# The first chunk of a projection made 384 tokens instead of 320, with five of the first loads issued by GpSimd

## The chip, the cores and the metric

The kernel runs on one core of one Trainium2 chip. The metric is the device time of one execution in microseconds (us). Before the change it is 463.41 us, the median of three runs (463.18 to 463.77).

## What is computed

One decoder layer over 1024 prompt tokens and 64 sample tokens (8 sequences of 8), 1088 tokens in all, with 1024 model columns. Cut to what matters here:

```python
def mixer_layer(x, conv_buf, S0, norm_g, w_in, ...):
    h = rms_norm(x, norm_g)
    proj = jnp.einsum('btd,de->bte', h, w_in.astype(h.dtype))
    a, gl, zc, q, k, v, zg, lr = jnp.split(proj, SPLIT_POINTS, axis=-1)
    u = a * jax.nn.sigmoid(gl)
    cv, new_buf = depthwise_causal_conv(u, conv_buf, conv_w, conv_b)
...
    out = jnp.einsum('bte,ed->btd', jnp.concatenate([cv, o], axis=-1), w_out.astype(x.dtype))
    return x + out, new_buf, S
```

The change concerns the start: the RMSNorm of x, and the first four of the projection's 128-column tiles, gl and a, each for convolution channels 0 to 127 and 128 to 255.

## The kernel before

**Tiling.** Tokens lie along the free dimension in three chunks, `CHUNKS = [(0, 384), (384, 384), (768, 320)]`; the last holds 256 prompt tokens and all 64 sample tokens. The 1024 model columns are eight groups of 128 partitions, k = 0 to 7. Each fp32 operand is split into a high and a low part (`hh` and `hl` for the normed x, `h_...` and `l_...` for weights), and a product is three matmuls: high by high, low by high, high by low. One weight tile over one chunk is so 8 x 3 = 24 matmuls into one PSUM bank (`proj_chunk`).

**The start.** `FIRST = 2`: the chunk of 320 tokens is taken first, and in a special way. Its x is multiplied by the norm's gain and split at once (`raw_split`, two instructions per k: one of ScalarE, one of VectorE), without the root mean square, which `rms_scale` works out beside it and which is multiplied onto the results afterwards. So TensorE can begin as soon as x for k = 0 and the first weights are there. Four weight tiles (gl and a for channel tiles 0 and 1; in the text gl0, a0, gl1, a1) are loaded in halves of four k each; the first half of each comes in two pieces of two k (128 KB each), the second half in one piece (256 KB). Loads of x, one per k, stand between them. The four matmul groups of this chunk are 96 matmuls. After it come chunks 0 and 1 with the same weights, 192 matmuls; they need the normed x, for which squares (ScalarE), sums (VectorE), a small matmul with a matrix of 1/1024 (`ms`), a logarithm and an exponential (`rs`, ScalarE), the multiplication (VectorE) and the split (both) must be done.

**Staging slots.** The staging tiles of the first halves take the four slots of the pool `wst`. Of the second halves, those of gl0 and a0 need such a slot again, so they wait until the first half's split has read it; those of gl1 and a1 are put into the pool `big` (`STAGE = 6`) and find free slots there.

**Order.** All instructions are recorded by `prog.add` with a cost, an engine and their dependencies, and a planner (`schedule`) replays them in a model of the chip. The instructions of each engine are then issued in the order of that plan, and the engines run them strictly in order. On the chip an instruction waits for the data it reads and for the slot it overwrites. `prog.hold` adds a dependency for the planner alone:

```python
        if self.hold:
            o.deps.add(self.last_pe if self.hold is True else self.hold)
            self.hold = False
```

It fixes when the plan places an instruction, and so its place in its engine's queue; no wait is issued for it (`issue` gives waits to slots alone, and the data's waits follow from what is read and written). In the plan a load by SyncE ends by bytes at 250 and later 350 GB/s, and an accumulating load by GpSimd ends 1000 + 5000 ns after its start.

**Loads.** All loads up to 340 us go through SyncE's queue (`SPq`), but for `par`, the 128 x 152 table of gains, biases and convolution weights, which ScalarE issues. GpSimd only writes constants until then. From 340 us on GpSimd issues 16 loads that add to what is there (`dma_add`).

Of the kernel before, what the change touches and what calls it, by code (L numbers as in the profile page):

```python
# [29 lines left out]
C_NG, C_BA, C_CW, C_CB, C_CG, C_CBT, C_BP, C_GG, C_EPS, NPAR = 0, 8, 10, 134, 138, 142, 146, 150, 151, 152  # L30
# [10 lines left out]
MT_COL = {"a": E_A, "gl": E_GL, "zc": E_ZC, "q": E_Q, "k": E_K, "zg": E_ZG}  # L41


FIRST = 2
STAGE = 6
LOW = 1 << 20
STATES_AT = 1
CN_LAST = 2
ADD_LAG = 5000
STICK = 60  # L50
SLACK = 500
SLACK_FROM = 45000
DVE_PACE = 1.05
DMA_SLACK = 2000
SLOW_TO = 4500
SQ_SUM = (2, 4, 8)
MARGIN = 20
NWARM = 9
STEP = 0
# [78 lines left out]
class Program:  # L138
# [51 lines left out]
    def schedule(self):  # L190
# [51 lines left out]
        while events:  # L242
# [18 lines left out]

            if same is not None and t > SLACK_FROM and same.prio < best.prio + STICK:
                best = same
# [72 lines left out]
def build(tc, A, O):  # L336
    nc = tc.nc
    ctx = ExitStack()
    V, S, G, T = nc.vector, nc.scalar, nc.gpsimd, nc.tensor
    prog = Program({"big": NBIG, "unit": NUNIT, "wst": NST, "wl": NW, "wh": NW, "ps": 8, "kT": 2, "S": 8, "ss": 9},  # L340
                   {"ps": 3, "unit": 8, "big": 2})
# [4 lines left out]
    def R(v):  # L346
        return v.ap() if isinstance(v, View) else v

    def act(out, in_, func, bias=None, scale=None, accum=None):
        def fn():  # L350
            kw = {}
            if bias is not None:
                kw["bias"] = R(bias)
            if scale is not None:
                kw["scale"] = R(scale)
            if accum is not None:
                kw["accum_out"] = R(accum)
            return S.activation(R(out), R(in_), func, **kw)  # L358
        extra = 93 * (isinstance(bias, View) + isinstance(scale, View)) + 90 * (accum is not None)
        base = 51 if in_.tile.tag == "ps" else 93  # L360
        prog.add("ACT", fn, [out, accum], [in_, bias, scale], out.n / 1.2 + base + extra, TABLES.get(func))

    def stt(out, a, s, b, op0, op1):
        return prog.add("DVE", lambda: V.scalar_tensor_tensor(R(out), R(a), R(s), R(b), op0, op1), [out], [a, s, b],  # L364
                 out.n / 0.96 + 67 + 62 * isinstance(s, View))

    def tt(out, a, b, op):
        return prog.add("DVE", lambda: V.tensor_tensor(R(out), R(a), R(b), op), [out], [a, b], out.n / 0.96 + 67)  # L368
# [29 lines left out]
    def dma(out, in_, late=False, eng="SP", small=False):  # L398
        v = out if isinstance(out, View) else in_
        if late:  # L400
            prog.hold = late
        q = nc.sync if eng == "SP" else S
        prog.add(eng, lambda: q.dma_start(R(out), R(in_)), [out], [in_], 0,  # L403
                 nbytes=v.n * 4 * (v.part[1] - v.part[0]) * (6 if small else 1))

    def dma_add(out, in_):

        prog.add("POOL", lambda: G.dma_start(R(out), R(in_), accum_op=ALU.add), [out], [in_], 1000,
                 nbytes=out.n * 4 * P, lag=ADD_LAG)

    def mm(ps, lhsT, rhs, start, stop, after=(), share=1):
        n, m = rhs.n, lhsT.n
        lag = 150 if m <= 64 and not R_DT(rhs) else 0
        c = max(n / 2.4 + 14, m / 1.2) if R_DT(rhs) else max(n / 1.2 + 2.5, m / 1.2) + max(n / 1.2 if m > 64 else 53, m / 1.2)
        o = prog.add("PE", lambda: T.matmul(R(ps), R(lhsT), R(rhs), start=start, stop=stop, skip_group_check=True),  # L415
                     [ps], [lhsT, rhs], c / share, lag=lag, kind=R_DT(rhs))
        o.deps.update(a for a in after if a is not None)
        return o
# [7 lines left out]
    with ctx:  # L426
# [9 lines left out]
        def VT(pool, tag, shape, dt, name):  # L436
            return View.of(Tile_(pool, tag, shape, dt, name))
# [4 lines left out]
        def un(name, dt=F32):  # L442
            return VT(unit, "unit", [P, 384], dt, name)

        def pt(name):
            return VT(psp, "ps", [P, 512], F32, name)

        def split(hi, lo, src):
            act(hi, src, AF.Copy)
            tt(lo, src, hi.bitcast(F32), ALU.subtract)  # L450

        par = VT(fixed, "par", [P, NPAR], F32, "par")
# [11 lines left out]
        def pc(i, n=1):  # L464
            return par[:, i:i + n]
# [23 lines left out]
        def x_load(c, ks=range(KT), late=False, eng="SP"):  # L489
            t0, n = CHUNKS[c]  # L490
            for k in ks:
                xk = rows("x", k, F32)[:, t0:t0 + n]
                dma(xk, A["xT"][:, k, t0:t0 + n], late, eng)
                xs[(c, k)] = xk
# [3 lines left out]
        def rows(name, k, dt):  # L498

            if (name, k) not in row_tiles:  # L500
                row_tiles[(name, k)] = bt(f"{name}{k}", dt)
            return row_tiles[(name, k)]

        def part(name, k, c):
            t0, n = CHUNKS[c]
            return rows(name, k, F32R)[:, t0:t0 + n]
# [3 lines left out]
        def raw_split(ks):  # L510

            for k in ks:
                g, xk = pc(C_NG + k), xs[(FIRST, k)]
                hi, lo = part("hh", k, FIRST), part("hl", k, FIRST)
                act(hi, xk, AF.Copy, scale=g)
                stt(lo, xk, g, hi.bitcast(F32), ALU.mult, ALU.subtract)
                raw[k] = hi, lo

        def rms_scale(c):
            n = CHUNKS[c][1]  # L520
            ms = pt(f"ms{c}")[:, :n]
            g = SQ_SUM[c]
            for k in range(KT):
                sq = un(f"sq{c}_{k}")[:, :n]
                act(sq, xs[(c, k)], AF.Square)
                if k % g == 0:
                    acc = sq
                else:
                    tt(acc, acc, sq, ALU.add)
                if k % g == g - 1:  # L530
                    mm(ms, one_d, acc, k == g - 1, k == KT - 1)
            rs[c] = un(f"rs{c}")[:, :n]
            act(rs[c], ms, AF.Ln, bias=eps)
            act(rs[c], rs[c], AF.Exp, scale=-0.5)

        def rms_split(c, wait=None):
            n = CHUNKS[c][1]
            for k in range(KT):
                xk = xs[(c, k)]
                if wait is not None:  # L540
                    prog.hold = wait
                stt(xk, xk, pc(C_NG + k), rs[c], ALU.mult, ALU.mult)
                hh[k][c], hl[k][c] = part("hh", k, c), part("hl", k, c)
                split(hh[k][c], hl[k][c], xk)
# [14 lines left out]
        def whalf_parts(kind, i, h, stage=None):  # L559

            name, src = f"{kind}{i}_{h}", A["w_in"][mt[(kind, i)]]
            st = VT(stage or wst, "big" if stage else "wst", [P, 4, P], F32, f"s_{name}")
            hi = VT(wh, "wh", [P, 4, P], F32R, f"h_{name}")
            lo = VT(wl, "wl", [P, 4, P], F32R, f"l_{name}")

            def piece(a, b, eng):
                dma(st[:, a:b, :], src[:, 4 * h + a:4 * h + b, :], eng=eng)
                split(hi[:, a:b, :], lo[:, a:b, :], st[:, a:b, :])

            return (hi, lo), piece  # L570
# [473 lines left out]
                mix_samples(4 + i, o[:, 256:n])  # L1044


        dma(par, A["par"], eng="ACT")
        w0, w1 = [[], []], [[], []]
        for h in range(2):
            parts_ = []  # L1050
            for w, kind, ct in ((w0[0], "gl", 0), (w0[1], "a", 0), (w1[0], "gl", 1), (w1[1], "a", 1)):
                tiles, piece = whalf_parts(kind, ct, h, big if 4 * h + len(parts_) >= STAGE else None)
                w.append(tiles)
                parts_.append(piece)

            n = 2 if h == 0 else 4
            for j in range(0, 4, n):
                for i, piece in enumerate(parts_):
                    if i < n:
                        k = 4 * h + j + i  # L1060
                        x_load(FIRST, range(k, k + 1))
                        raw_split(range(k, k + 1))
                    piece(j, j + n, "SP")
        rms_scale(FIRST)
        x_load(0)
        x_load(1, late=True)
        rms_scale(0)
        rms_split(0)
        rms_scale(1)
        for ct, w in enumerate((w0, w1)):  # L1070
            gl_chunk(ct, w[0], FIRST, True)
            a_chunk(ct, w[1], FIRST, True)
        rms_split(1)
        w_rank = gate_load()
        begun = None
        for c in (0, 1):
            for ct, w in enumerate((w0, w1)):
                gl_chunk(ct, w[0], c)
                begun = begun or prog.last_pe
                a_chunk(ct, w[1], c)  # L1080
# [436 lines left out]
```

## Time and profile before

| | us |
|---|---|
| median of three runs | 463.41 |
| the profiled execution, its own time | 463.69 |
| its span in the trace | 461.9 |
| TensorE busy | 451.9 (98%) |
| VectorE busy | 393.1 (85%) |
| ScalarE busy | 306.6 (66%) |
| GpSimd busy | 19.1 (4%) |
| bytes moved | 43.26 MB, mean 94 GB/s |

The span runs from the first to the last instruction; 1.8 us of the execution's time lie around it. A matmul's end is modelled and overlaps the next one's start, so TensorE's idle time is read from the distances between the starts of matmuls: in an undisturbed row they follow at one fixed distance for each width, and what is over that is idle. PE is TensorE, PEld its weight loads, DVE is VectorE, ACT is ScalarE, POOL is GpSimd, SP is SyncE; a name with q behind it is the queue of loads that the engine issues.

### The profile page before, as it was taken

How to read it: one execution, taken by the hardware profiler on the slowest of the kernel's cores; microseconds unless marked ns; L12 is line 12 of the kernel's file. 1: busy time of each engine (PE TensorE's matmuls, PEld its weight loads, DVE VectorE, ACT ScalarE, POOL GpSimd, SP SyncE). 2: the span in 40 equal slices, each digit the busy share in tenths (PEclk: the TensorE clock that was granted, in tenths of full speed). 3: DMA queues.
4: the chain of work that ended last, by engine and by line, in shares of the span. 5: the costliest groups of instructions: out<-in, count | busy, mean ns of one | idle time of the engine just before them, and what ended most of it. 6: DMA issues, size and time to landing. Idle time of an engine off the chain costs nothing.

```text
span 461.9 us, 7604 instructions
## 1 busy us (share of the span) xinstructions
PE 451.9 (98%) x2728; PEld 413.8 (90%) x2728; DVE 393.1 (85%) x629; ACT 306.6 (66%) x782; POOL 19.1 (4%) x38
## 2 busy tenths in 40 slices
PE   8899999999999999999999999999999999999994
PEld 8699989999888899898999899999999988888783
DVE  5789999999999999999999899953549847988684
ACT  7767979363643623658866797653899548879554
POOL 1000000000000000000000000000000023220000
PEclk9999999999999999999999999999999999999998
DMA  7935340141200040003211211011235474476744
GB/s 214 328 126 104 67 146 15 47 68 35 57 0 1 23 153 9 2 8 107 70 57 48 82 58 45 26 66 64 77 81 183 118 196 68 78 166 152 270 151 182
DMA packets 36485, 43.26 MB, mean 94 GB/s; under 512 B 13024, under 2 KB 21344, under 8 KB 36448
## 3 DMA queue, kind: packets, MB, share of 16 engines
q1 hardware_dynamic: 33856, 38.25, 26.5%
q0 software_dynamic: 2304, 4.20, 5.7%
q8 instruction: 21, 0.34, 0.3%
q10 hardware_dynamic: 288, 0.34, 0.2%
q14 instruction: 16, 0.13, 0.1%
HBM read 36.58 MB, written 6.19 MB: 93 GB/s over the span
## 4 chain that ended last, share of the span: by engine, by line
PE 91%; DMA 3%; ACT 2%; DVE 1%; SPq 1%; issue 1%
PE ya L415 11%; PE p_zc L415 10%; PE p_zg L415 10%; PE pv L415 10%; PE p_gl L415 9%; PE p_a L415 9%; PE p_k L415 5%; PE pw L415 5%; PE p_q L415 5%; PE yc L415 5%; PE po L415 2%; DMA x<-in_xT 2%; PE pys L415 2%; DMA s_a<-in_w_in 1%; SPq L403 1%; PE px L415 1%
## 5 line engine op out<-in xcount | busy, mean ns | idle before, releaser
L364 DVE SCALAR_TENSOR_TENSOR cv<-u,par,cv 128x1024 f32<-128x1024 f32 x120 | 150.9, 1278 | 0.2
L415 PE MATMUL p_gl<-hh,h_gl 128*128 128x384 f32 (+1 forms) x96 | 32.2, 336 | 2.0 <-ACT h_gl L358 1.3
L358 ACT ACTIVATE pr<-us,par 128x64 f32<-128x64 f32 x124 | 32.3, 343 | 0.0
L415 PE MATMUL p_gl<-hh,l_gl 128*128 128x384 f32 (+1 forms) x96 | 32.3, 336 | 0.0
L415 PE MATMUL p_gl<-hl,h_gl 128*128 128x384 f32 (+1 forms) x96 | 31.7, 331 | 0.2 <-DVE hl L364 0.2
L415 PE MATMUL p_zc<-hh,h_zc 128*128 128x384 f32 (+1 forms) x96 | 31.7, 330 | 0.0
L415 PE MATMUL p_a<-hl,h_a 128*128 128x384 f32 (+1 forms) x96 | 31.6, 329 | 0.0
L415 PE MATMUL p_zc<-hl,h_zc 128*128 128x384 f32 (+1 forms) x96 | 31.5, 328 | 0.0
L415 PE MATMUL p_zc<-hh,l_zc 128*128 128x384 f32 (+1 forms) x96 | 31.5, 328 | 0.0
L415 PE MATMUL p_zg<-hl,h_zg 128*128 128x384 f32 (+1 forms) x96 | 31.5, 328 | 0.0
L415 PE MATMUL p_zg<-hh,l_zg 128*128 128x384 f32 (+1 forms) x96 | 31.4, 327 | 0.0
L415 PE MATMUL p_zg<-hh,h_zg 128*128 128x384 f32 (+1 forms) x96 | 31.4, 327 | 0.0
L415 PE MATMUL p_a<-hh,h_a 128*128 128x384 f32 (+1 forms) x96 | 31.3, 326 | 0.0
L415 PE MATMUL p_a<-hh,l_a 128*128 128x384 f32 (+1 forms) x96 | 31.2, 326 | 0.0
L415 PE MATMUL pv<-h_v,hl 128*128 128x512 f32 x64 | 25.0, 390 | 0.0
L415 PE MATMUL pv<-l_v,hh 128*128 128x512 f32 x64 | 24.9, 390 | 0.0
L415 PE MATMUL pv<-h_v,hh 128*128 128x512 f32 x64 | 24.9, 389 | 0.0
L415 PEld LDWEIGHTS p_gl<-hh,h_gl 128*128 128x128 f32 x96 | 18.0, 188 | 3.6 <-ACT h_gl L358 2.1
L415 PEld LDWEIGHTS p_gl<-hh,l_gl 128*128 128x128 f32 x96 | 18.0, 188 | 1.3 <-DVE l_gl L368 0.4
L415 PEld LDWEIGHTS p_gl<-hl,h_gl 128*128 128x128 f32 x96 | 18.0, 188 | 0.7 <-DVE hl L364 0.4
L368 DVE TENSOR_TENSOR o<-o,zg 128x384 f32<-128x384 f32 (+1 forms) x12 | 6.2, 534 | 14.5 <-ACT zg L358 14.5
L415 PEld LDWEIGHTS p_zc<-hh,h_zc 128*128 128x128 f32 x96 | 18.1, 188 | 0.3 <-issue 0.2
(345 smaller groups left out, 1284.2 us busy)
## 6 DMA issues: line engine op xcount, KB each, us to landing
xr<-in_x SPq DMA_DIRECT2D x16, 256.0 KB, 4.8
out_y<-xr SPq DMA_DIRECT2D x15, 256.0 KB, 2.1
x<-in_xT SPq DMA_DIRECT2D x16, 192.0 KB, 5.3
T<-in_w_out POOLq DMA_DIRECT2D x12, 256.0 KB, 5.1
s_v<-in_wv SPq DMA_DIRECT2D x16, 128.0 KB, 2.8
s_zc<-in_w_in SPq DMA_DIRECT2D x8, 256.0 KB, 2.6
s_zg<-in_w_in SPq DMA_DIRECT2D x8, 256.0 KB, 2.6
s_gl<-in_w_in SPq DMA_DIRECT2D x6, 256.0 KB, 4.8
```

Of the source, the lines that this page charges most:

```text
L358: return S.activation(R(out), R(in_), func, **kw)
L364: return prog.add("DVE", lambda: V.scalar_tensor_tensor(R(out), R(a), R(s), R(b), op0, op1), [out], [a, s, b], out.n / 0.96 + 67 + 62 * is ...
L368: return prog.add("DVE", lambda: V.tensor_tensor(R(out), R(a), R(b), op), [out], [a, b], out.n / 0.96 + 67)
L403: prog.add(eng, lambda: q.dma_start(R(out), R(in_)), [out], [in_], 0, nbytes=v.n * 4 * (v.part[1] - v.part[0]) * (6 if small else 1))
L415: o = prog.add("PE", lambda: T.matmul(R(ps), R(lhsT), R(rhs), start=start, stop=stop, skip_group_check=True), [ps], [lhsT, rhs], c / share ...
```

## The change

Chunk 0 (384 tokens) is taken first, then chunk 1, then chunk 2 (320 tokens, with the samples). The table `par` is loaded in two parts: its first 8 columns (the gains) by ScalarE as before, the other 144 by GpSimd. The second halves of the four weight tiles are loaded by GpSimd as well, with `prog.hold` on the VectorE half of `raw_split` for k = 1. These loads have a cost of 1000 ns and a lag of `LOAD_LAG = 3500` ns in the plan. `SQ_SUM`, how many squares are summed before an `ms` matmul, keeps its values by turn: 8 for the first chunk, 2 for the second, 4 for the third.

```diff
-FIRST = 2
+FIRST = 0
+NEXT, THIRD = 1, 2
...
+LOAD_LAG = 3500
...
-SQ_SUM = (2, 4, 8)
+SQ_SUM = (8, 2, 4)
...
         q = nc.sync if eng == "SP" else S
+        if eng == "POOL":
+            prog.add(eng, lambda: G.dma_start(R(out), R(in_)), [out], [in_], 1000,
+                     nbytes=v.n * 4 * (v.part[1] - v.part[0]), lag=LOAD_LAG)
+            return
...
-        dma(par, A["par"], eng="ACT")
+        dma(par[:, 0:C_BA], A["par"][:, 0:C_BA], eng="ACT")
...
                         raw_split(range(k, k + 1))
-                    piece(j, j + n, "SP")
+                        if k == 1:
+                            started = prog.ops[-1]
+                            prog.hold = started
+                            dma(par[:, C_BA:], A["par"][:, C_BA:], eng="POOL")
+                    if h == 1:
+                        prog.hold = started
+                    piece(j, j + n, "POOL" if h == 1 else "SP")
         rms_scale(FIRST)
-        x_load(0)
-        x_load(1, late=True)
-        rms_scale(0)
-        rms_split(0)
-        rms_scale(1)
+        x_load(NEXT)
+        x_load(THIRD, late=True)
+        rms_scale(NEXT)
+        rms_split(NEXT)
+        rms_scale(THIRD)
...
-        rms_split(1)
+        rms_split(THIRD)
...
-        for c in (0, 1):
+        for c in (NEXT, THIRD):
```

## Rows read from the trace of the kernel before

**Rows 1.** The page, parts 1 and 2: busy time of the engines with their share of the span and their instructions, and TensorE's busy tenths in 40 slices of 11.5 us.

```profile
PE 451.9 (98%) x2728; PEld 413.8 (90%) x2728; DVE 393.1 (85%) x629; ACT 306.6 (66%) x782; POOL 19.1 (4%) x38
...
PE   8899999999999999999999999999999999999994
```

**Rows 2.** The view of waits for TensorE over the whole span, but for the warm-up: who waited for whom, us in total, times, the longest.

```profile
PE p_gl L415 <- ACT h_gl L358: 1.3, 2, 0.9
...
PE p_gl L415 <- ACT hh L358: 0.6, 2, 0.4
PE p_gl L415 <- DVE hl L364: 0.2, 1, 0.2
```

**Rows 3.** The view of windows, the first 25 us in stretches of 5: the stretch and its length, busy us (and instructions) of PE, PEld, DVE, ACT and POOL, the granted TensorE clock as a share of full speed, the DMA engines' busy share, GB/s moved.

```profile
0.00:5.00 5.00, 3.89 (x19) 3.71 (x19) 0.77 (x3) 2.51 (x4) 1.97 (x11) 1.00 0.54 152
5.00:10.00 5.00, 4.63 (x27) 4.01 (x28) 4.29 (x11) 4.39 (x12) 0.00 (x0) 1.00 0.89 262
10.00:15.00 5.00, 4.07 (x26) 3.55 (x26) 4.03 (x10) 3.79 (x9) 0.00 (x0) 1.00 0.87 273
15.00:20.00 5.00, 4.56 (x26) 3.83 (x27) 4.48 (x9) 4.69 (x11) 0.00 (x0) 1.00 1.00 347
20.00:25.00 5.00, 5.00 (x26) 3.74 (x25) 1.78 (x4) 3.08 (x7) 0.00 (x0) 1.00 1.03 364
```

**Rows 4.** The same view for 26 to 60 us, the same columns.

```profile
26.00:60.00 34.00, 33.60 (x190) 32.66 (x189) 33.70 (x70) 27.63 (x81) 0.31 (x1) 1.00 0.37 86
```

**Rows 5.** The timeline of TensorE's matmuls: start, modelled length, what it is; in brackets the idle time before it and what ended it.

```profile
4.97 0.41 PE L415 MATMUL p_gl<-hh,h_gl 128*128 128x320 f32 x1
...
6.88 0.31 PE L415 MATMUL p_gl<-hh,l_gl 128*128 128x320 f32 x1
...
7.62 0.31 PE L415 MATMUL p_a<-hh,h_a 128*128 128x320 f32 x1
...
12.89 0.31 PE L415 MATMUL p_a<-hl,h_a 128*128 128x320 f32 x1
14.11 0.41 PE L415 MATMUL p_gl<-hh,h_gl 128*128 128x320 f32 x1 [0.90 <-ACT h_gl L358]
...
16.85 0.41 PE L415 MATMUL p_gl<-hh,h_gl 128*128 128x320 f32 x1 [0.44 <-ACT h_gl L358]
...
25.85 0.31 PE L415 MATMUL p_a<-hh,l_a 128*128 128x320 f32 x1
26.56 0.44 PE L415 MATMUL p_gl<-hh,h_gl 128*128 128x384 f32 x1 [0.40 <-ACT hh L358]
...
40.63 0.33 PE L415 MATMUL p_gl<-hh,l_gl 128*128 128x384 f32 x1
...
44.79 0.33 PE L415 MATMUL p_gl<-hh,h_gl 128*128 128x384 f32 x1
```

**Rows 6.** The timeline of ScalarE: the first split of x, that of x for k = 2, the splits of the first two second halves of weights, and the second split of chunk 0's x group; columns as in Rows 5.

```profile
3.69 0.56 ACT L358 ACTIVATE hh<-x,par 128x320 fp32r<-128x320 f32 x1 [1.66 <-DMA par<-in_par]
...
7.45 0.56 ACT L358 ACTIVATE hh<-x,par 128x320 fp32r<-128x320 f32 x1 [0.18 <-DMA x<-in_xT]
...
13.42 0.63 ACT L358 ACTIVATE h_gl<-s_gl 128x512 fp32r<-128x512 f32 x1 [0.79 <-DMA s_gl<-in_w_in]
...
15.29 0.63 ACT L358 ACTIVATE h_a<-s_a 128x512 fp32r<-128x512 f32 x1 [0.42 <-DMA s_a<-in_w_in]
...
26.00 0.51 ACT L358 ACTIVATE hh<-x 128x384 fp32r<-128x384 f32 x1
```

**Rows 7.** The timeline of SyncE's queue: the four loads of second halves (256 KB each), of which the first two and the last stand here. Columns: time of issue, how long the issue took, what.

```profile
8.16 0.43 SPq L403 DMA_DIRECT2D s_gl<-in_w_in  x1
...
9.11 0.43 SPq L403 DMA_DIRECT2D s_a<-in_w_in  x1
...
11.22 0.33 SPq L403 DMA_DIRECT2D s_a<-in_w_in  x1
```

**Rows 8.** The timeline of GpSimd: the last constants that it writes at the start.

```profile
1.86 0.52 POOL L393 MEMSET vs<- 64x512 f32 x1
2.45 0.18 POOL L393 MEMSET u<- 128x30 f32 x2
```

**Rows 9.** Loads: from the page's part 6 (what, queue, number, KB each, median us from issue to landing), then from the view of the tile T (GpSimd's accumulating loads: ns of one issue, minimum, median and maximum, first and last start; and the landing of all T loads).

```profile
x<-in_xT SPq DMA_DIRECT2D x16, 192.0 KB, 5.3
T<-in_w_out POOLq DMA_DIRECT2D x12, 256.0 KB, 5.1
```

```profile
L408 POOL DMA_DIRECT2D T<-in_w_out x12: 862/936/1927, 340.4 to 402.8; - x12
...
DMA to landing us min/median/max: 2.9/4.5/7.8
```

**Rows 10.** The views of the tiles x and cv: the squares, VectorE's multiplication and the split's low part for the normed x, all three chunks (ns of one, minimum, median and maximum, first and last start), and the first convolution instruction of each channel tile.

```profile
L358 ACT ACTIVATE sq<-x x24: 453/508/528, 4.2 to 29.7; 128x384 f32<-128x384 f32 x16, 128x320 f32<-128x320 f32 x8
L364 DVE SCALAR_TENSOR_TENSOR x<-x,par,rs x24: 542/611/619, 24.7 to 51.8; 128x384 f32<-128x384 f32 x16, 128x320 f32<-128x320 f32 x8
...
L368 DVE TENSOR_TENSOR hl<-x,hh x24: 480/550/559, 26.5 to 54.1; 128x384 fp32r<-128x384 f32 x16, 128x320 fp32r<-128x320 f32 x8
```

```profile
L374 DVE TENSOR_SCALAR cv<-u,par x4: 803/809/812, 56.9 to 184.9; 128x1024 f32<-128x1024 f32 x4
```

## The prediction

> **What bounds the kernel now.** I read the page first: TensorE is busy 98% of the span, and its slices are full but for the first two and the last [rows 1]. The view of waits says who stops it: apart from the warm-up its waits for data sum to 2.1 us, all on the gl matmuls of the start [rows 2]. The windows from 26 us on show TensorE full but for the 0.4 us at their beginning [rows 4]. So only what happens before about 27 us can change the time, unless an order later on is upset; the rest is TensorE's own work.
>
> In the first 27 us I count idle time by starts [rows 5]. Width 320: 36 steps from 7.62 to 12.89, 0.1464 us each. Width 384: 24 steps from 40.63 to 44.79, 0.1733 each. TensorE begins at 4.97. Over that pace it loses
> - 1.18 us up to 6.88 (five steps take 1.91, five at pace 0.73): x for k = 1 and the first weight pieces trickle in;
> - 2.06 us from 12.89 to 16.85 (13 steps take 3.96, at pace 1.90): the second halves are late. Their splits stand in ScalarE's row just before, and waited for the loads [rows 6];
> - 0.56 us from 25.85 to 26.56: the next chunk's split [rows 6] isn't there.
>
> Together 3.80 us. The 96 matmuls of the first chunk are 96 x 0.1464 = 14.05, so of the 21.03 us from 4.97 to 26.00 there remain 21.03 - 14.05 - 1.18 - 2.06 = 3.74 for the `ms` matmuls among them.
>
> The loads behind this: the DMA engines are 0.87 to 0.89 busy from 5 to 15 us and move 262 to 273 GB/s; only from 15 us on is it 347 and more [rows 3]. Added up: 0.76 MB by 5 us, 2.07 by 10, 3.43 by 15, 5.17 by 20. By program order x for k = 2 ends at 1.09 MB, which this sum passes at 6.3; its split started at 7.45 [rows 6]. A load can so be used about 1.1 us after its bytes' turn.
>
> **The change, part by part.** *384 tokens first.* The work that the first weights feed grows by 96 x (0.1733 - 0.1464) = 2.58 us; the third chunk gives the same back, so TensorE's total stays. What it buys is cover: the first halves alone now last 48 x 0.1733 = 8.3 us instead of 7.0. Its price is 8 x 32 KB = 0.26 MB more before the chunk is complete, 0.26 / 0.265 = 1.0 us of loading; ScalarE has 0.05 more per square [rows 10] and about as much per split, 0.9 us in all, VectorE some 0.06 for each of 15 instructions, 0.9. Both were idle for some microseconds in this time (VectorE 3.2 of 5 us after 20) [rows 3], and the third chunk gives it back.
>
> *Second halves from GpSimd.* SyncE loses the four issues from 8.16 to 11.22 [rows 7], so x for k = 7 and the next chunk move up by four issues of 0.43. Each GpSimd issue costs 0.86 to 1.93 us (median 0.94), and landing takes 2.9 to 7.8 us [rows 9]. When does it begin? The hold on k = 1 is no wait: the zeroing of `u` has a hold on a matmul of the first gl group, none of which starts before 4.97, yet it ran at 2.45 [rows 5, 8]. So I expect GpSimd to issue the rest of `par` at about 2.4, and gl1 and a1, whose slots are free, at about 3.3 and 4.3, four to five microseconds before SyncE did; gl0 and a0 wait for slots (were the hold real, all would start after 6.6, when the second low part of x is done). Ends: landing 4.5 after issue puts gl1 at 7.8, 7.8 puts it at 11.1; TensorE wants it after the first halves, at 4.97 + 8.3 + 1.18 = 14.4. Either way the 2.06 us of late second halves go, but not free: 0.6 MB now share the engines with the first pieces of x and weights at 3.5 to 8 us. If GpSimd's queue takes half, SyncE has moved about 1.0 instead of 1.5 MB by 8 us; x for k = 2 ends at 1.12 MB and is usable at 9.5 instead of 7.45. The matmuls of k = 0 and 1 with the first pieces, 24 x 0.1733 = 4.2 us from 4.97 with the old 1.18 idle, last to 10.3; k = 2 split and ready at 10.6 costs 0.3 to 0.8. I take 0.5 (ends 0 and 2.0). gl0 and a0 follow when their slots are read, some 11 and 12 us, and share with x for k = 5 to 7; usable at 16 to 17.5, wanted at about 19 and later. x for k = 6 and 7 may come short by 0.3 (ends 0 and 1).
>
> By the Trainium skill, DMA: Bandwidth & Descriptors, section Queues, rings and completion order, each DMA engine goes round between the queues that have work, packet by packet. No row here shows two queues loaded at the start; without that rule, first come first served, the 0.5 would be about 0 and the sum 0.5 better. It is the rule that speaks against this change, and the third rival below is what it would do.
>
> *`par` in two parts.* The first split waited for `par` [rows 6]; now x itself is waited for, 20% larger. Ends: 0.2 earlier to 0.2 later, I take 0. The other columns are wanted by `rs` at 20 us and later, hidden.
>
> *The next chunk.* Bytes up to its last x rise by 0.26 MB, or 0.26 / 0.347 = 0.75 us at the rate then [rows 3]; its split would come at about 26.7 to 27.3. TensorE's first chunk now ends at 4.97 + 16.64 + 3.74 + idle (1.18 + 0.5 + 0.3) = 27.3, so the 0.56 shrinks to about 0 (ends 0 and 0.6).
>
> *After 27 us.* VectorE is full from 26 to 60 us [rows 4], its last part of x splits is at 54.1 and its first convolution at 56.9 [rows 10]. TensorE will want its work up to 2 us earlier than now. That the convolution, filler with a far due time, starts after the splits leaves about the 3 us needed; 0 taken, 1 at worst. The samples come with the third chunk, in convolutions that need all three anyhow: 0.
>
> **How the numbers follow.** Idle before 3.80, idle after 1.18 + 0.5 + 0.3 + 0 = 2.0: 1.8 us saved. The profiled execution took 463.69, 0.28 over the median: 463.69 - 1.8 = 461.9, and 461.6 as a median. A measurement can tell about 0.2%, 0.93 us, from no change: below 462.5 is faster, above 464.3 slower.
>
> **The rivals.**
> - *All gaps go.* Engines that stood at 0.87 have room, and the early traffic costs nothing: idle after is 1.0 or less, saved 2.8: 460.6. For it: SyncE's queue alone leaves 12% of the engines idle at 5 to 15 us [rows 3]. Against: 1.18 of the gaps are before any of this helps. Chance 0.10.
> - *x becomes what is late.* The second halves are there, but x for k = 4 to 7, larger and behind half a queue, is not, and in-order TensorE stays idle at 13 to 17 us by half of the old 2.06, with 0.5 more at the next chunk or behind VectorE: saved about 0.5: 462.9. For it: the same engines move the same bytes. Against: TensorE has 1.3 us more of first-half work. Chance 0.18.
> - *The change doesn't do what it says.* GpSimd's loads land no earlier than SyncE's did (late slots, up to 7.8 us to land), and only the wider chunk acts: it covers 1.3 of 2.06, loses 0.3 by its bytes: saved 1.0: 462.4. Chance 0.10.
> - *Slower: the start starves.* GpSimd's two big loads go ahead of the first x: 0.6 MB at 265 GB/s is 2.3 us before k = 1 and 2 can be taken, and TensorE, idle most of 5 to 9 us just after its warm-up, is granted the lower clock, 1.2 GHz, where matmuls take twice as long: some 3 us at that level lose 1.5, and the planned order misses again at 13 us for 1. Saved 3.80 - (1.18 + 2.3 + 1.5 + 1.0) = -2.2 at the full price, about -1 at half of the last two: 464.4 to 465.6. It decides when TensorE's early idle time passes 1.18 + 2.6. Against: the clock stayed at 1.00 through 1.2 us without a matmul [rows 3, 5], and x for k = 0 and 1 are issued before GpSimd's first big load. Chance 0.10.
> - *The forecast*, 461.6, with 461.0 to 462.3: chance 0.52.
>
> Faster: 0.52 + 0.10 + 0.05 of x late + 0.06 of the fourth = 0.73. Same: 0.13 + 0.04 + 0.03 of the starved start = 0.20. Slower: 0.07. The range goes from the case of no gaps to that of late x with its margin: 460.6 to 463.2.
>
> **What would show it.** Right: GpSimd issues loads from 2.4 us; second-half splits don't wait for loads, or not at 13 us; matmuls at 0.173 steps from 13 to 17; TensorE begins the next chunk at 27 to 27.5 after 96 matmuls of 384. The early gap up to 10 us is 1.2 to 2.2. Wrong: GpSimd's first big load after 6.5; a granted clock under 1.00; a gap over 0.6 at the end of the first chunk; new waits of TensorE for VectorE between 40 and 65 us, or a different last part of the span.

## The result, and the profile after

After the change the kernel takes 466.32 us (median of five runs, 465.37 to 467.11) against 463.41 before (five runs by now, 463.09 to 464.01): a ratio of 1.0064, 95% interval 1.0052 to 1.0077. It is slower by 2.9 us, above the whole range of the prediction. The profiled execution took 466.32 us, its span 464.5 (before: 463.69 and 461.9).

The page's parts 1 and 2, of after; they answer to [rows 1]:

```profile
PE 453.8 (98%) x2728; PEld 415.4 (89%) x2728; DVE 393.5 (85%) x629; ACT 307.2 (66%) x782; POOL 21.5 (5%) x43
...
PE   7999999999999999999999999999999999999994
...
PEclk9899999999999999999999999999999999999999
```

Hardly anything is to be seen: a 7 for an 8 in TensorE's first slice, and an 8 in the second slice of the clock (PEclk, the granted clock in tenths). Where the loss sits is read from two groups of matmuls that lie later and do the same in both kernels, `pl` and `ya` (view of the tiles; the last two times are the first and the last start). Before:

```profile
L415 PE MATMUL pl<-x,lr_w x64: 392/393/417, 64.0 to 67.5; 128*32 128x272 f32 x64
...
L415 PE MATMUL ya<-p1b,p1a x48: 388/389/398, 371.3 to 382.0; 128*128 128x512 f32 x48
```

After:

```profile
L421 PE MATMUL pl<-x,lr_w x64: 392/392/417, 66.7 to 70.2; 128*32 128x272 f32 x64
...
L421 PE MATMUL ya<-p1b,p1a x48: 389/389/398, 374.1 to 384.8; 128*128 128x512 f32 x48
```

TensorE is 2.7 us late at 64 us and 2.8 late at 371: the whole loss arises at the start and is only carried along. The first 25 us in windows, after, columns as in [rows 3]:

```profile
0.00:5.00 5.00, 3.94 (x19) 3.94 (x19) 0.94 (x3) 2.62 (x4) 3.54 (x12) 1.00 0.54 144
5.00:10.00 5.00, 4.39 (x20) 3.27 (x18) 2.16 (x6) 2.17 (x5) 0.00 (x0) 1.00 0.96 313
10.00:15.00 5.00, 3.13 (x12) 2.98 (x12) 4.18 (x10) 4.46 (x11) 1.25 (x4) 0.75 0.89 284
15.00:20.00 5.00, 5.00 (x28) 5.00 (x27) 4.13 (x9) 4.00 (x9) 0.00 (x0) 0.91 0.99 343
20.00:25.00 5.00, 4.92 (x24) 3.87 (x23) 3.74 (x7) 3.96 (x10) 0.00 (x0) 1.00 0.66 219
```

From 5 to 10 us the DMA engines move more than before (313 against 262 GB/s [rows 3]) and yet ScalarE and VectorE have half their former work: the bytes that come are the wrong ones. From 10 to 15 us TensorE does 12 matmuls instead of 26, and the granted clock is 0.75. GpSimd's, ScalarE's and TensorE's timelines of after show why (answering to [rows 5, 6, 8]):

```profile
2.34 0.71 POOL L406 DMA_DIRECT2D par<-in_par  x1
3.03 0.57 POOL L406 DMA_DIRECT2D s_gl<-in_w_in  x1
3.58 0.54 POOL L406 DMA_DIRECT2D s_a<-in_w_in  x1
12.91 0.54 POOL L406 DMA_DIRECT2D s_gl<-in_w_in  x1 [8.78 <-DVE l_gl L370]
14.24 0.54 POOL L406 DMA_DIRECT2D s_a<-in_w_in  x1 [0.80 <-DVE l_a L370]
```

```profile
7.56 0.42 ACT L360 ACTIVATE h_gl<-s_gl 128x256 fp32r<-128x256 f32 x1 [0.89 <-DMA s_gl<-in_w_in]
9.50 0.42 ACT L360 ACTIVATE h_a<-s_a 128x256 fp32r<-128x256 f32 x1 [1.52 <-DMA s_a<-in_w_in]
10.54 0.61 ACT L360 ACTIVATE hh<-x,par 128x384 fp32r<-128x384 f32 x1 [0.63 <-DMA x<-in_xT]
...
18.61 0.63 ACT L360 ACTIVATE h_gl<-s_gl 128x512 fp32r<-128x512 f32 x1 [0.99 <-DMA s_gl<-in_w_in]
...
21.09 0.63 ACT L360 ACTIVATE h_a<-s_a 128x512 fp32r<-128x512 f32 x1 [1.02 <-DMA s_a<-in_w_in]
```

```profile
4.93 0.67 PE L421 MATMUL p_gl<-hh,h_gl 128*128 128x384 f32 x1
...
9.72 0.34 PE L421 MATMUL p_gl<-hh,l_gl 128*128 128x384 f32 x1
11.93 0.44 PE L421 MATMUL p_gl<-hh,h_gl 128*128 128x384 f32 x1 [1.87 <-ACT h_gl L360]
...
12.38 0.38 PE L421 MATMUL p_a<-hh,h_a 128*128 128x384 f32 x1
12.57 0.52 PE L421 MATMUL p_a<-hl,h_a 128*128 128x384 f32 x1
12.89 0.52 PE L421 MATMUL p_gl<-hh,l_gl 128*128 128x384 f32 x1
...
15.77 0.42 PE L421 MATMUL p_a<-hh,h_a 128*128 128x384 f32 x1
...
31.21 0.34 PE L421 MATMUL p_gl<-hh,h_gl 128*128 128x384 f32 x1
31.86 0.44 PE L421 MATMUL p_gl<-hl,h_gl 128*128 128x384 f32 x1 [0.31 <-DVE hl L370]
```

SyncE's seventh load is x for k = 2:

```profile
3.55 0.43 SPq L409 DMA_DIRECT2D x<-in_xT  x1
```

GpSimd issues 512 KB (gl1, a1) at 3.03 and 3.58 us without a wait, as forecast; the first of the two is ahead of x for k = 2. After that the last first-half pieces come late (ScalarE waits 0.89 and 1.52 us for them), and x for k = 2 is split at 10.54 instead of 7.45 [rows 6]. From 9.72 to 11.93 TensorE starts nothing: 2.21 us less one step of 0.173 are 2.04 us idle. Then ten steps of 0.32 us follow at half the clock. gl0 and a0, which wait for slots, are issued at 12.91 and 14.24 and split at 18.61 and 21.09. The first chunk ends at 31.21.

### The profile page after: what moved, and what is told of

The parts are those of the page before. It is cut to its first block, busy times and chain, and to the rows that moved or that the text cites. A ratio compares the mean times of both kernels' runs of the same rounds, so it can differ in the third digit from the quotient of the medians.

```text
span 464.5 us, 7616 instructions
## 1 busy us (share of the span) xinstructions
PE 453.8 (98%) x2728; PEld 415.4 (89%) x2728; DVE 393.5 (85%) x629; ACT 307.2 (66%) x782; POOL 21.5 (5%) x43
## 4 chain that ended last, share of the span: by engine, by line
PE 91%; DMA 4%; DVE 1%; ACT 1%; issue 1%; SPq 1%; DVEq 0%; ACTq 0%
PE ya L421 11%; PE p_zc L421 10%; PE p_zg L421 10%; PE pv L421 10%; PE p_gl L421 9%; PE p_a L421 8%; PE p_q L421 5%; PE p_k L421 5%; PE pw L421 5%; PE yc L421 5%; DMA x<-in_xT 2%; PE po L421 2%; PE pys L421 2%; DMA s_a<-in_w_in 1%; PE pa L421 1%; PE px L421 1%
## 5 line engine op out<-in xcount | busy, mean ns | idle before, releaser
L421 PE MATMUL p_a<-hh,l_a 128*128 128x384 f32 (+1 forms) x96 | 32.2, 336 | 0.0
L360 ACT ACTIVATE v<-pv 128x512 f32<-128x512 f32 x8 | 4.8, 599 | 22.7 <-PE pv L421 21.4
L421 PEld LDWEIGHTS p_gl<-hl,h_gl 128*128 128x128 f32 x96 | 18.3, 191 | 1.3 <-DVE hl L370 0.8
L421 PEld LDWEIGHTS p_a<-hh,h_a 128*128 128x128 f32 x96 | 18.3, 191 | 0.2
```

## The experiments

All ratios are to before, with 95% intervals. Milestones are the first `pl` matmul (before 64.0 us, after 66.7) and the split of x for k = 2 (7.45, 10.54). The theory: the two big loads that don't wait take the DMA engines from x and from the first pieces. The rivals: the wide chunk costs it, or GpSimd as an issuer.

**The wide chunk alone** (all loads on SyncE, `par` whole):

```diff
-        dma(par[:, 0:C_BA], A["par"][:, 0:C_BA], eng="ACT")
+        dma(par, A["par"], eng="ACT")
...
-                            dma(par[:, C_BA:], A["par"][:, C_BA:], eng="POOL")
...
-                    piece(j, j + n, "POOL" if h == 1 else "SP")
+                    piece(j, j + n, "SP")
```

> The changed kernel with all first loads issued by SyncE again and the table par in one load by ScalarE; the first chunk stays 384 tokens. Theory 1 (traffic: the two big loads that GpSimd issues at 3.0 and 3.6 us take the engines from the first pieces): the loss goes and the wider chunk covers part of the late second halves, 462.0 to 463.4 us, no gap over 0.6 us before 12 us and a granted clock of 1.00. Theory 2 (width: x loads that are 20% larger make x for k = 2 and 3 late): 465 to 466.5 us, and the gap at 10 us is still 1.5 us or more.

462.50 us, 0.9979 [0.9970, 0.9988]; `pl` at 62.0; the gap at 13 us is 0.46 us instead of 1.07. The wide chunk is a gain, and the loss is gone.

**GpSimd's loads alone** (the table's second part among them; 320 tokens first as before):

```diff
-FIRST = 0
-NEXT, THIRD = 1, 2
+FIRST = 2
+NEXT, THIRD = 0, 1
...
-SQ_SUM = (8, 2, 4)
+SQ_SUM = (2, 4, 8)
```

> The changed kernel with the last 320 tokens first again; the second halves and most of par stay with GpSimd. Theory 1 (traffic): the first pieces are late as in the changed kernel, 465 to 466.5 us, with a gap of 1.5 us or more near 9 to 11 us. Theory 2 (width): 462 to 463.4 us and no such gap.

466.93 us, 1.0075 [1.0059, 1.0090]. In the profiled execution, a long one of 468.27 us, TensorE stands 3.51 us before k = 2, the granted clock falls to 0.51 from 14 to 16 us, and `pl` is at 69.4. The loads are the harm, and a greater one where the narrower chunk has TensorE out of work at 8.4 us instead of 9.9.

**Only the table by GpSimd** (wide chunk, second halves by SyncE), run twice:

```diff
-                    piece(j, j + n, "POOL" if h == 1 else "SP")
+                    piece(j, j + n, "SP")
```

> The changed kernel with the second halves issued by SyncE again; the 144 other columns of par stay with GpSimd, the first chunk stays 384 tokens. Theory 1 (traffic): 74 KB at 2.3 us are little; the first split of x starts at 3.5 instead of 3.85 us (width_alone), and the time is that of width_alone or up to 0.4 us less, 0.997 to 0.999 of the kernel before. If the table's part, or GpSimd's queue being active at all, is what slows the start: 1.002 or more.

> The best version so far once more: 384 tokens first, 144 columns of the table issued by GpSimd, all weight loads by SyncE. Expected 461.4 to 462.2 us, 0.9957 to 0.9974 of before, if its earlier 0.9962 was no luck; above 0.998 it is no better than the wide chunk alone.

461.83 us, 0.9962 [0.9948, 0.9977], and 461.80 us, 0.9960 [0.9947, 0.9972]. It beats both kernels; against it the second halves by GpSimd cost 3.9 to 4.8 us (1.0046 or 1.0064, after's two ratios, less 0.9961). TensorE of the second run at its largest gap:

```profile
13.35 0.34 PE L421 MATMUL p_a<-hh,h_a 128*128 128x384 f32 x1
14.50 0.44 PE L421 MATMUL p_gl<-hh,h_gl 128*128 128x384 f32 x1 [0.82 <-ACT h_gl L360]
```

0.98 us are idle where before had 2.06, and the next chunk begins at 27.69, where the forecast had 27.3.

**The table by GpSimd, 320 tokens first:** `FIRST = 2` in the kernel above.

> 320 tokens first as before, all weight loads by SyncE, but the table in two parts as in the change (8 columns by ScalarE, 144 by GpSimd). If the table's split is worth what the pair of the wide chunk alone (0.9979) and the wide chunk with the table (0.9962) suggests, 0.998 to 0.9988 of before, with the first split of x up to 0.4 us earlier than before's 3.69. If the table brings nothing by itself (x is late anyhow, as the forecast took it): 0.9993 to 1.0007.

464.13 us, 1.0012 [1.0002, 1.0022], above either expectation; first split at 3.46 instead of 3.69, `pl` at 63.9. By itself the split table gains nothing. That with the wide chunk it ran at 0.996 and the wide chunk alone at 0.998 (the intervals overlap) is not seen at the start (`pl` at 62.1 and 62.3 against 62.0), but at `ya`, at 369.3 and 369.4 against 369.7; here `ya` is at 371.8 against 371.3 before. What arises between the two milestones stays open.

**A real wait.** GpSimd first copies a column of `hl` for k = 1 into a tile that nothing reads:

```diff
+                            seen = VT(fixed, "seen", [P, 1], F32, "seen")
+                            low = raw[1][1][:, 0:1].bitcast(F32)
+                            prog.add("POOL", lambda: G.tensor_copy(R(seen), R(low)), [seen], [low], 60)
                             dma(par[:, C_BA:], A["par"][:, C_BA:], eng="POOL")
```

> The changed kernel in which GpSimd first copies one column of the low part of x for k = 1, so that its four big loads really wait for it (about 6.6 us); the copy is not used. Theory 1 (traffic): x for k = 2 is usable at 7.5 to 9 instead of 10.5 us, the gap at 10 us falls under 1 us, the clock stays at 1.00: 461.8 to 463.8 us. Theory 2 (width) or a theory that GpSimd's queue is slow whenever it starts: 465.5 us or more.

464.19 us, 1.0014 [1.0004, 1.0024], worse than expected. The loads are issued at 7.39, 7.94, 9.86 and 11.19; x for k = 2 is on time (7.38), but now x for k = 4 is the one that waits, on ScalarE:

```profile
12.57 0.62 ACT L360 ACTIVATE hh<-x,par 128x384 fp32r<-128x384 f32 x1 [1.76 <-DMA x<-in_xT]
```

TensorE stands 2.27 us at 13.5 instead of 2.04 at 9.7, and the granted clock is 0.67 from 16 to 18 us and 0.50 from 18 to 20. The harm moved on to what was next in the other queue.

**One early load** (gl1 at 3.04; the same copy stands ahead of a1, at 7.34):

```diff
+                    if h == 1 and i == 3:
+                        seen = VT(fixed, "seen", [P, 1], F32, "seen")
+                        low = raw[1][1][:, 0:1].bitcast(F32)
+                        prog.add("POOL", lambda: G.tensor_copy(R(seen), R(low)), [seen], [low], 60)
                     if h == 1:
```

> The changed kernel in which only gl1's second half (256 KB) is issued by GpSimd without a wait; a1's and the others follow a copy that waits for the low part of x for k = 1, at 6.6 us or later. Theory 1 (traffic, by bytes): the gap near 10 us is about half of the changed kernel's 2.0, and 1.002 to 1.005 of the kernel before. If the gap comes from a fixed cost of GpSimd's early queue: as the changed kernel, 1.006.

464.77 us, 1.0023 [1.0011, 1.0034]; the gap before k = 2 is 1.12 us: half the bytes, about half of 2.04. The clock stays at 1.00. What ScalarE waits for here is the first piece of a1; x for k = 2 is split right behind it without a wait. And the gap is not the only limit:

```profile
9.57 0.42 ACT L360 ACTIVATE h_a<-s_a 128x256 fp32r<-128x256 f32 x1 [1.26 <-DMA s_a<-in_w_in]
9.93 0.62 ACT L360 ACTIVATE hh<-x,par 128x384 fp32r<-128x384 f32 x1
```

```profile
19.29 0.44 PE L421 MATMUL p_gl<-hh,h_gl 128*128 128x384 f32 x1 [1.39 <-ACT h_gl L360]
```

gl0's second half, issued at 12.30 when its slot was free, holds TensorE up to 19.29, about as long as in the second trace of the change below (19.38). So `pl` in this execution (a long one, 465.99 us) is at 66.4 in spite of the smaller gap.

**No early load but by slots.** `STAGE = 8`: all four second halves wait for slots of `wst`, and GpSimd issues them from 10.33 to 12.70.

> The changed kernel with all four second halves in the staging pool of four slots (STAGE = 8), so that all of GpSimd's big loads wait until a first half has been split, 9 us or later. Theory 1: the first halves and x for k = 2 and 3 come as in width_alone, no gap before 12 us; x for k = 4 to 7 or the second halves may be late by 1 us, 0.998 to 1.002 of the kernel before. If the loss has nothing to do with when GpSimd's loads start: 1.006.

466.05 us, 1.0046 [1.0031, 1.0060], not the 1 expected. Nothing is missing before 12 us, then TensorE stands 2.33 us at 14.5 for gl0 (the clock stays at 1.00) and 1.82 at 25.5 for the sums of squares. Too late costs about as much as too early.

**Two by GpSimd, two by SyncE** (GpSimd issues gl0 and a0, at 9.92 and 11.23; gl1 and a1 stand in SyncE's row):

```diff
-                    if h == 1:
+                    late = h == 1 and i < 2
+                    if late:
                         prog.hold = started
-                    piece(j, j + n, "POOL" if h == 1 else "SP")
+                    piece(j, j + n, "POOL" if late else "SP")
```

> The changed kernel in which GpSimd issues only the second halves of gl0 and a0, which wait for their slots until 10 us or later; those of gl1 and a1 are with SyncE as in the kernel before. Theory 1 (the two loads without a wait are the harm): no starved start, clock 1.00 to 13 us, 0.996 to 0.9995 of the kernel before. If loads of GpSimd do harm whenever they run beside SyncE's: 1.002 or more, as in the run held.

462.57 us, 0.9977 [0.9966, 0.9988]: as the wide chunk alone. So GpSimd as an issuer did no harm here, where its loads come when they are needed.

**The hole filled.** Twelve matmuls of 384 columns, whose results are overwritten, stand in TensorE's row just ahead of gl0 with k = 2:

```diff
             i = o.fn().ins
...
+            if o is self.fill_at:
+                self.fill()
...
+                    def fill():
+                        for _ in range(NFILL):
+                            T.matmul(R(spare), R(w0[0][0][0][:, 1, :]), R(raw[1][0]), start=True, stop=True,
+                                     skip_group_check=True)
```

> The changed kernel with 12 more matmuls of 384 columns just ahead of the first one that uses x for k = 2, where TensorE stands idle for 2.0 us; their result is overwritten. Theory 3 (the lower clock from 12.4 to 15.9 us follows from that idle time and costs 1.5 us by itself): granted clock 1.00 throughout, 464.6 to 465.1 us. If the clock's fall has another reason or is hidden by a later wait: 466 us, or slower by up to 0.3.

464.90 us, 1.0023 [1.0014, 1.0031]; the clock is 1.00 throughout, `pl` at 65.4. The numbers are those expected, but they do not show that filling held the clock: in the next run it stays without filling. Nor is the gain the clock's alone: k = 2 begins at 11.42 here, 0.5 us before after.

**The change once more**, unaltered, for a second trace.

> The changed kernel once more, for its trace. If what it showed is the kernel's own and not one execution's: x for k = 2 split at 10.0 to 11.0 us, a gap of TensorE of 1.7 to 2.4 us before it, the granted clock at 1.2 GHz for 2 to 4 us behind it, and 1.005 to 1.008 of before.

465.67 us, 1.0046 [1.0031, 1.0061]. x for k = 2 is split at 10.67; TensorE's row and the window from 10 to 15 us:

```profile
9.79 0.34 PE L421 MATMUL p_gl<-hh,l_gl 128*128 128x384 f32 x1
12.05 0.45 PE L421 MATMUL p_gl<-hh,h_gl 128*128 128x384 f32 x1 [1.92 <-ACT h_gl L360]
12.33 0.34 PE L421 MATMUL p_gl<-hl,h_gl 128*128 128x384 f32 x1
...
19.38 0.44 PE L421 MATMUL p_gl<-hh,h_gl 128*128 128x384 f32 x1 [0.72 <-ACT h_gl L360]
```

```profile
10.00:15.00 5.00, 3.08 (x17) 2.81 (x17) 4.11 (x10) 4.39 (x12) 1.13 (x4) 1.00 0.88 267
```

The gap is the kernel's own (2.09 us); the expected fall of the clock did not come. So nearly the same gap was followed by the lower clock in one execution and not in another. What that cost is read from k = 2's first matmul to the first of `pl`: 54.74 us in after (11.93 to 66.67), 53.99 here (12.05 to 66.04) and 53.94 with the hole filled (11.42 to 65.36), so about 0.8 us. It isn't the 1.5 us of its ten slow steps, since a TensorE that doesn't lose them stands 0.89 us at 18.3 for gl0.

**The early loads in SyncE's own queue.** gl1 and a1 are issued by SyncE behind its sixth load, at 3.55 and 4.03 us, all other rows unchanged:

```diff
         order = self.schedule()
+        sync = [o for o in order if o.eng == "SP"]
+        at = order.index(sync[5]) + 1
+        for o in self.moved:
+            order.remove(o)
+            order.insert(at, o)
+            o.eng, at = "SP", at + 1
```

> The kernel after, but for its two early second halves (gl1 and a1, 256 KB each): SyncE issues them behind its sixth load, at about 3.5 and 4.0 us, instead of GpSimd at 3.0 and 3.6; the order on every other engine is the same, and gl0, a0 and the table stay on GpSimd. Theory (what harms is 0.52 MB of unneeded bytes put ahead of x for k = 2, whichever queue they stand in): x for k = 2 is split at 9.5 us or later, TensorE idles 1 to 2.5 us before k = 2, the time is 1.003 to 1.008 of before. Rival (a second queue, GpSimd's, is the harm, one queue in order is none): the split of k = 2 starts by 8.5 us, the gap is under 0.6 us and the time is 0.996 to 1.000.

464.79 us, 1.0028 [1.0015, 1.0040]. x for k = 2 is split at 9.28, the gap before it is 1.17 us, the clock stays: the theory, a little under its numbers.

```profile
9.28 0.62 ACT L367 ACTIVATE hh<-x,par 128x384 fp32r<-128x384 f32 x1 [1.68 <-DMA x<-in_xT]
```

```profile
10.66 0.44 PE L429 MATMUL p_gl<-hh,h_gl 128*128 128x384 f32 x1 [1.00 <-ACT h_gl L367]
```

By this run the bytes ahead of x account for 1.8 of the 3.1 us (1.7 to 1.8 against the 7.49 to 7.62 of the wide chunk without early loads); 1.3 are left. The places are not quite the same: behind the sixth load the two leave the first pieces alone (a1's is split at 7.19, in after at 9.50). What each queue had moved by 8 us (queue, packets, MB, time as a share of 16 engines; q1 is SyncE's, q0 GpSimd's), in this run and in after:

```profile
q1 hardware_dynamic: 1197, 1.51, 67.4%
q0 software_dynamic: 32, 0.07, 2.9%
```

```profile
q1 hardware_dynamic: 996, 1.10, 47.8%
q0 software_dynamic: 142, 0.45, 18.9%
```

Both sums are near 1.55 to 1.58 MB: a second queue brings no more bytes, it only changes whose.

**The early loads in pieces.** GpSimd issues gl1 and a1 as two loads of 128 KB each (3.03 to 4.63 us):

```diff
+                G.dma_start(R(out[:, 0:2, :]), in_[:, 0:2, :])
+                return G.dma_start(R(out[:, 2:4, :]), in_[:, 2:4, :])
```

> The kernel after, but GpSimd issues each of its two early second halves (gl1, a1) as two loads of 128 KB, so 512 KB in 4 loads; everything else is in the same place. In the trace of after a 256 KB load of GpSimd makes 80 packets, one of SyncE 144, and between 6 and 8 us GpSimd's queue moved 0.33 MB in 102 packets, SyncE's 0.25 MB in 211. Theory (engines take turns between queues by packet, so the queue with the larger packets takes the larger share, and that is why GpSimd's loads delay x for k = 2 by 3.1 us where the same bytes in SyncE's own queue delay it by 1.8): with packets half as large GpSimd's queue moves at most 0.26 MB from 6 to 8 us, x for k = 2 is split by 10.0 us, TensorE's gap before it is 1.0 to 1.6 us, and the time is 1.003 to 1.0055 of before. Rival (the share does not go by packets, the delay comes from GpSimd's queue as such): split at 10.4 us or later, a gap of 1.9 or more, 1.0055 or above. The two more issues (0.55 us each) put the last bytes back by 1.1 us, which may by itself take up to 0.3 us off the gap.

465.07 us, 1.0043 [1.0029, 1.0058]; x for k = 2 is split at 8.78, the gap is 1.12 us, and from 6 to 8 us GpSimd's queue moves 0.21 MB in 81 packets, SyncE's 0.28 in 243. All numbers expected came, but the reason behind them is not borne out: the queue's packets over the whole run rose by only 32, that is 48 per 128 KB load after 80 per 256 KB. If 16 of each load's packets are small ones, the rest are of 4 KB in both kernels. So it was probably not smaller packets; the loads were issued over 2.1 us instead of 1.1.

**The early loads by ScalarE** (a second queue with SyncE's 144 packets a load; issued at 3.65 and 4.02 behind the first split, which puts TensorE's first matmul at 5.42): the same edit with `"ACT"` and the place behind the first `hh`.

> The kernel after, but for its two early second halves (gl1, a1), which ScalarE issues behind the first split of x, at about 4.0 and 4.5 us; order and place of all else as in after. ScalarE's queue is a second queue like GpSimd's, but if its loads look like SyncE's they come in 144 packets per 256 KB, not 80. The split of x for k = 2 is the reading: 10.54 us in after (GpSimd's queue), 9.28 with the same bytes in SyncE's own queue, 7.45 before. Theory (GpSimd's larger packets take the larger turn): 8.6 to 9.6 us. Rival (any second queue holds x back beyond its bytes): 10.2 or later. ScalarE's two issues also put its first weight split and TensorE's first matmul back by some 0.9 us; the time, of which this is a part, is 1.003 to 1.008 of before by either.

465.25 us, 1.0035 [1.0018, 1.0052]. x for k = 2 is split at 9.43, as with SyncE's own queue:

```profile
9.43 0.61 ACT L367 ACTIVATE hh<-x,par 128x384 fp32r<-128x384 f32 x1 [1.43 <-DMA x<-in_xT]
```

So a second queue as such doesn't make the last 1.1 us, at least with loads issued this late: x for k = 2 was issued at 3.56, ahead of both, where in after it was issued behind the first and just ahead of the second. That GpSimd's larger packets make them is not shown by it either: ScalarE's queue had moved 0.22 MB by 8 us, GpSimd's in after 0.38 beside the table, and in the run before this one a slower pace, probably with the same 4 KB packets, was enough. Pace, packets or time of issue stays open.

The time says nothing of the gap, for TensorE was slow here. From 7.87 to 10.43 its matmuls follow at 0.32 us, the pace of the lower clock in after, and 1.2 us longer than 8 steps of 0.1733, though the view of windows gives a granted clock of 1.00 from 7 to 10 us:

```profile
8.83 0.53 PE L429 MATMUL p_gl<-hh,h_gl 128*128 128x384 f32 x1
9.15 0.53 PE L429 MATMUL p_a<-hh,l_a 128*128 128x384 f32 x1
```

## Why the prediction was wrong, step by step

TensorE begins at 4.93, and the forecast's own sum, made against the profiled execution, can be laid beside the trace (us):

| term | forecast | after |
|---|---|---|
| over the pace up to 9.7 us | 1.18 | 1.84 (17 steps of 0.1733 in 4.79) |
| before k = 2 | 0.5 | 2.04 |
| lower clock, 11.93 to 16.03 | 0 | 1.67 (14 steps in 4.10) |
| x for k = 6, 7 | 0.3 | 0 |
| `ms` with the gaps around it | 3.74 | 4.09 (what remains up to 31.21) |
| next chunk | 0 | 0.48 (31.21 to 31.86) |
| sum | 5.72 | 10.12 |

The difference of 4.4 is that of the times, 466.32 against 461.9.

*The step that failed* is in "Second halves from GpSimd": "k = 2 split and ready at 10.6 costs 0.3 to 0.8. I take 0.5 (ends 0 and 2.0)"; measured 2.04. What stands ahead of it was right: issue without a wait, and "SyncE has moved about 1.0 instead of 1.5 MB by 8 us", measured 1.10. Three things built on it were wrong.

- The lag. That a load is usable 1.1 us after its bytes' turn was taken from a kernel with one queue at work. x for k = 2 ends at 1.11 MB by the order of SyncE's queue (three loads of x, four pieces); after passes that at about 8.1 us and uses it 2.5 us later, in both traces. The first piece of a1, which ends at 0.92 MB, was passed at about 7.0 and split at 9.50, as late. With the same bytes in SyncE's queue the turn of x for k = 2 ends at 1.64 MB, at about 8.4, and the lag is 0.9. So its split, put at 9.5, began at 10.54: 1.04 us.
- The way from there. The weight split for k = 2 stands behind that split and its square in ScalarE's row, and TensorE could go on at 11.93, 1.39 us later and not 1.1: 0.29 us.
- The work ahead, "24 x 0.1733 = 4.2 us". Only 18 matmuls stand ahead of k = 2 in TensorE's row; the six of a1 for k = 0 and 1 come behind (from 12.38 on), though their weights were split by 10.38. With 0.66 more lost on the way, TensorE ran out of work at 9.9, not 10.3: 0.4 us. Ahead of k = 2 those six might have filled up to 1.0 us of the gap, an estimate from these rows; no run tries it.

With the 0.3 between 10.3 and 10.6 that makes up the 2.04.

*The clock* at 0 was wrong for this execution and right for the second trace, where the table's 1.67 would be 0 and 0.89 come in at 18.3. *The rest of `ms`* moved since gl0 and a0 got their slots at 12.91 and 14.24 (forecast 11 and 12) and were split at 18.61 and 21.09 (16 to 17.5 for both): squares stand behind them on ScalarE, and the sums behind those.

*Right:* the hold is no wait; gl1 and a1 are in time (their splits wait for no load); what the wide chunk is worth, 462.4 in the rival "The change doesn't do what it says", 462.50 measured when it alone acts (by its total; no trace shows its two terms, 1.3 covered and 0.3 lost, to be right); the table's split at about 0 at the start (TensorE begins at 4.93 instead of 4.97); the loss or gain is settled before 60 us.

*The rivals.* "Slower: the start starves", with 464.4 to 465.6 and a chance of 0.10, comes nearest; 466.32 lies above it too. Its early idle of 1.18 + 2.3 was 3.88, past its point of 3.78; its clock term of 1.5 was 1.67. But in the second trace the early idle is 3.96 and the clock stays, so that point does not decide. Its second miss at 13 us did not come; in place of it the `ms` matmuls and the next chunk lost 0.83. Its low chance rested on x for k = 0 and 1 being issued first. They were in time; k = 2 was the victim.

By the Trainium skill, DMA: Bandwidth & Descriptors, section Queues, rings and completion order, one copy is split over up to 16 engines, and completion isn't first in, first out even for one issuing engine. That would let x for k = 2 wait for its slowest engine after 1.11 MB had passed on the whole, which fits the lag of 2.5 us; no run here shows single engines, so what lengthens the lag stays argued. The same section's rule, that an engine goes round between its queues packet by packet, agrees in that both queues moved at once, and in that ScalarE's two loads, issued behind x for k = 2, held it back all the same (9.43); from 6 to 8 us it was 102 packets of GpSimd's (0.33 MB) to 211 of SyncE's (0.25 MB), one to two and not one to one. That both had work on every engine all that time, which a count of one to one would need, no row shows.

The forecast drew two things from this rule that do not hold. Without it, "first come first served", the 0.5 would not have been about 0: GpSimd's first load was issued at 3.03, ahead of x for k = 2 at 3.55, and with the bytes ahead of x in SyncE's one queue TensorE still stood 1.17 us. And the "third rival", which the rule is said to give, is by the list the one where GpSimd's loads land no earlier; x held back by a second queue is in "x becomes what is late" and "the start starves".

## What to carry to other kernels

Where the DMA engines are nearly full, moving loads to a second queue added no bytes here but reordered them: list what is wanted next, and keep loads wanted later from being issued ahead of it, since a planner's hold that issues no wait doesn't, and a real wait can move the harm on to the next load. Price a load behind two queues not by its bytes' turn plus the lag of one queue, and count in the engine's own order what stands ahead of the work that waits. Test a change of several parts part by part: here one part was worth a good 0.2 to 0.4%, and another took more than all of it away.

## What was not expected of the hardware

- A plain load of 128 x 512 took GpSimd 0.54 to 0.57 us to issue, where its accumulating loads took 0.86 and more [rows 9].
- A 256 KB load made 80 packets from GpSimd's queue and 144 from SyncE's or ScalarE's.
- A gap of 2.04 us was followed by 1.2 instead of 2.4 GHz (granted clock 0.50 from 13 to 15 us) in one execution, and one of 2.09 us by 2.4 GHz throughout in another execution of the same kernel. In other kernels it fell after gaps of 2.27 us (a real wait) and 3.51 (GpSimd's loads alone) and stayed after one of 2.33 (no early load but by slots).
- With the early loads by ScalarE, matmuls of 384 columns followed at 0.32 us from 7.87 to 10.43, though the granted clock is given as 1.00 there.
